# Half of the pooling branch's gates as a third unit of seven products; two recurrence chunks on the un-normalised input; the input's sums later in the list

## The chip, the core and the metric

The kernel runs on one core of a Trainium2 chip. The metric is the device time of one launch in microseconds (us); the kernel before has a median of 901.03 us over three runs (900.64 to 901.3). A core has a matmul engine (TensorE, PE in the profile, with PEld for its weight loads), a vector engine (VectorE, DVE), an engine for activation functions (ScalarE, ACT), a general one (GpSimd, POOL), a queue engine (SyncE, SP) and DMA engines. Each works through a list of its own in order; semaphores hold them together.

## The reference, cut

One layer of a hybrid encoder for 512 tokens of width 1024, all in float32:

```
h = rms_norm(x, norm_mix)
u_pool, u_lru, q, k, v, g_logits = split(h @ w_in)            # 5 x 1024 and 3 x 1024 columns
gates = sigmoid(g_logits + b_gate)                            # three branches x 1024
y_pool = causal means of u_pool over windows 2, 4, 8, 16, less the token, a linear map per group
xc = conv_b + sum_k conv_w[k] * u_lru[t - 3 + k]              # RG-LRU
r = sigmoid(xc @ w_rg + b_rg); i = sigmoid(xc @ w_ig + b_ig)  # block-diagonal
log_a = -8 * r * softplus(-lambda); a = exp(log_a); b = sqrt(-expm1(2 * log_a)) * (i * xc)
y_lru[t] = a[t] * y_lru[t-1] + b[t]
y_sb = stick-breaking attention of 8 heads on rms-normed q, k and on v
merged = sum over branches: gates[branch] * (y_branch @ w_branch[branch])
x = x + merged @ w_out
x = x + (silu(n @ w_ffn_gate) * (n @ w_ffn_up)) @ w_ffn_down,  n = rms_norm(x, norm_ffn)
```

rms_norm scales each token by one number. That number can be left out of a product with `w_in` and multiplied to the result after.

## The kernel before

Channels lie on the 128 partitions and tokens along the rows, so a chunk of 256 output channels is one PSUM pair of tiles 128 x 512. Each float32 operand is split in two parts of fewer bits (`hi` rounded by a ScalarE copy, `lo` the VectorE difference), and each product is three matmuls: hi x hi, hi x lo, lo x hi. `hu` is the input times `norm_mix` in two parts, not yet normalised; `HH` and `HL` (`hn`) are the two parts of the normalised h. `rb` is the row of the tokens' scales, broadcast over partitions.

Weights come in a fixed list, `specs`. A direct chunk of 256 columns has two entries, one for each half of the contraction, with 24 matmuls of 512 columns each. `split_w` takes a raw tile to `whi` (ScalarE, line 110) and `wlo` (VectorE, line 111), three buffers each: the split of entry n needs all matmuls of entry n - 3 done. A Tile scheduler writes each engine's list from the program's order and from priorities (`EARLY`, `AHEAD`); `keep_in_program_order` fixes an instruction against that. PSUM has four pairs of tiles (`pb`).

The stages are:

1. Gates of branch 0 (pooling), chunks 0 and 1, on `hu`, while the input lands; then its chunks 2 and 3, also on `hu`, while the scales and `hn` are made (`norm_h`). Their PSUM results are multiplied by `rb` and go through a sigmoid (`gate_store`).
2. The recurrence. `lru_chunk(c)` is 48 matmuls on `hn` (`ps_lru`), a convolution over time on VectorE, a split of its result, 12 matmuls `lg` with the two small matrices, eight sigmoids on ScalarE (`lr`, `li`), then tanh, exponential and square root (`lru_exp`), and on VectorE `lru_decay`, `lru_input`, `lru_scan`, `lru_store`. Four such chunks stand between the direct gate chunks of branch 1, `gate1(0..3)`. The small pieces are put in a list `bg` by `step`, and each half of a chunk's matmuls takes pieces from it by `tick`.
3. V, K, Q by seven products of half size instead of eight (Winograd's form of Strassen). `ORDER` is the order of the seven, and T1 to T4 are the sums of blocks of h that they need (`diff_h`, then `split_t`, parts `hT1h` and so on; `prepare_t` lists these eight steps). Product 11 of V lands in `ps_q`; ScalarE takes a snapshot `r` of it (`snap`, line 811), and S2 then adds onto the same PSUM tile.
4. Gates of branch 2 by seven products, two units of 512 channels each: 7 x 24 matmuls of 256 columns (`product`, line 287, `gate_done`), from the same sums T1 to T4. Weights of these units are held in eight buffers `qw`, and sums of them are made by accumulating DMAs and VectorE.
5. Pooling, attention and the branches' projections, which read the gates back from DRAM; the output projection; the FFN.

The work behind stage 4 isn't touched, but for the address from which the first branch reads two chunks of gates.

## Time and profile before

| | |
|---|---|
| three runs | 900.64, 901.03, 901.3 us |
| profiled execution | 900.73 us, of it 899.0 us from the first to the last instruction |
| TensorE's granted clock | 1.000 |
| TensorE busy | 893.4 us of the span, 99% |
| VectorE busy | 732.3 us, 81% |
| ScalarE busy | 523.2 us, 58% |

A line of the profile's timeline reads: start in us, length in us, engine, line of the kernel, operation, output<-inputs, shapes, xcount, and in brackets the idle time before it and what ended that. `whi<-raw` is a weight split. A matmul's length holds its way through the array, so the pitch between starts is what it costs. Groups of neighbouring alike instructions may be shown as one line with a count.

### The profile page before, as it was taken

To read this page: it belongs to the slowest core of one execution; us is meant where nothing else is said; L and a number is where in the kernel's file an instruction comes from. 1 tells how busy PE (TensorE), PEld (TensorE's weight loads), DVE (VectorE), ACT (ScalarE), POOL (GpSimd) and SP (SyncE) were. 2 spreads that over 40 slices of the span, in tenths; PEclk is the share of its full clock that TensorE was granted. 3 is DMA by queue.
4 is the path that set the end of the run, shared out by engine and by line. 5 is a ranking of instruction groups with operands and counts; after the bars stand their busy time and mean duration, and the time that the engine had idled before them with its cause. 6 is when DMAs were issued, how large, how long until landed. Compare 5 with 4: busy or idle time off the path is not lost.

```text
span 899.0 us, 14052 instructions
## 1 busy us (share of the span) xinstructions
PE 893.4 (99%) x5491; PEld 794.2 (88%) x5491; DVE 732.3 (81%) x922; ACT 523.2 (58%) x722; POOL 86.3 (10%) x126
## 2 busy tenths in 40 slices
PE   9999999999999999999999999999999999999998
PEld 6888778788899888888888988889999999989998
DVE  7897897988786599967887696699888888799764
ACT  7554989556856556555664544454555555664532
POOL 1110002232332101000001100000000000101200
PEclk9999999999999999999999999999999999999999
DMA  9585347789682785734736865245543333866842
GB/s 337 147 303 156 115 127 215 234 286 242 181 260 71 233 235 190 220 118 141 223 91 152 184 177 170 94 131 152 141 117 95 111 102 125 225 167 122 180 99 94
DMA packets 116579, 151.98 MB, mean 169 GB/s; under 512 B 8096, under 2 KB 90016, under 8 KB 116512
## 3 DMA queue, kind: packets, MB, share of 16 engines
q1 hardware_dynamic: 104416, 107.30, 37.7%
q0 software_dynamic: 11952, 43.52, 20.6%
q8 instruction: 43, 0.70, 0.3%
q10 hardware_dynamic: 144, 0.26, 0.1%
q14 instruction: 24, 0.20, 0.1%
HBM read 130.61 MB, written 18.87 MB: 166 GB/s over the span
## 4 chain that ended last, share of the span: by engine, by line
PE 95%; DVE 2%; ACT 2%; issue 1%; DMA 0%; SPq 0%; DVEq 0%; ACTq 0%
PE ps_y L287 11%; PE ps_x L287 8%; PE ps_q L798 7%; PE ps_dy L287 5%; PE ps_dx L287 4%; PE ps_br L278 3%; PE ps_br L279 3%; PE ps_br L280 3%; PE ps_gate L701 2%; PE ps_bY L1238 2%; PE ps_gy L287 2%; PE ps_gate L280 2%; PE ps_bX L1238 2%; PE ps_gx L287 2%; PE ps_gate L279 2%; PE ps_gate L278 2%
## 5 line engine op out<-in xcount | busy, mean ns | idle before, releaser
L110 ACT ACTIVATE whi<-raw 128x1024 fp32r<-128x1024 f32 x73 | 77.2, 1058 | 85.3 <-PE ps_out L279 17.0
L111 DVE TENSOR_TENSOR wlo<-raw,whi 128x1024 fp32r<-128x1024 f32 x73 | 89.1, 1220 | 32.9 <-ACT whi L110 32.9
L111 DVE TENSOR_TENSOR wlo<-qw,whi 128x1024 fp32r<-128x1024 f32 x48 | 58.6, 1222 | 20.8 <-ACT whi L110 20.5
L110 ACT ACTIVATE whi<-qw 128x1024 fp32r<-128x1024 f32 x48 | 50.8, 1057 | 33.1 <-PE ps_q L798 18.6
L1403 ACT ACTIVATE wh_S<-w_S 128x1024 fp32r<-128x1024 f32 x36 | 38.2, 1064 | 35.5 <-PE ps_y L287 22.4
L1404 DVE TENSOR_TENSOR wl_S<-w_S,wh_S 128x1024 fp32r<-128x1024 f32 x36 | 43.8, 1220 | 6.2 <-ACT wh_S L1403 6.2
L1403 ACT ACTIVATE wh<-w 128x1024 fp32r<-128x1024 f32 x27 | 28.8, 1066 | 30.3 <-issue 11.9
L1494 POOL DMA_DIRECT2D dw<-in_w_down_dram x16 | 13.5, 846 | 325.9 <-DVE wl L1404 248.2
L1404 DVE TENSOR_TENSOR wl<-w,wh 128x1024 fp32r<-128x1024 f32 x27 | 32.9, 1220 | 10.0 <-ACT wh L1403 10.0
L1403 ACT ACTIVATE whdS<-dw 128x1024 fp32r<-128x1024 f32 x16 | 17.0, 1064 | 24.4 <-PE ps_dy L287 13.2
L1404 DVE TENSOR_TENSOR wldS<-dw,whdS 128x1024 fp32r<-128x1024 f32 x16 | 19.6, 1224 | 12.9 <-ACT whdS L1403 12.9
L1054 DVE TENSOR_TENSOR_SCAN E<-K,ahead 128x512 f32<-128x512 f32 (+3 forms) x32 | 25.3, 812 | 4.4 <-ACT K L1050 4.4
L278 PE MATMUL ps_br<-yHH,whi 128*128 128x512 f32 x64 | 25.3, 395 | 0.0
L278 PE MATMUL ps_lru<-HH,whi 128*128 128x512 f32 x64 | 25.2, 394 | 0.0
L278 PE MATMUL ps_br<-yph,whi 128*128 128x512 f32 x64 | 25.2, 394 | 0.0
L278 PE MATMUL ps_pool<-HH,whi 128*128 128x512 f32 x64 | 25.2, 393 | 0.0
L279 PE MATMUL ps_br<-ypl,whi 128*128 128x512 f32 x64 | 25.0, 391 | 0.0
L280 PE MATMUL ps_gate<-HH,wlo 128*128 128x512 f32 x64 | 25.0, 391 | 0.0
L278 PE MATMUL ps_gate<-HH,whi 128*128 128x512 f32 x64 | 25.0, 391 | 0.0
L280 PE MATMUL ps_br<-yph,wlo 128*128 128x512 f32 x64 | 25.0, 391 | 0.0
L279 PE MATMUL ps_br<-yHL,whi 128*128 128x512 f32 x64 | 25.0, 390 | 0.0
L279 PE MATMUL ps_pool<-HL,whi 128*128 128x512 f32 x64 | 25.0, 390 | 0.0
(717 smaller groups left out, 3426.3 us busy)
## 6 DMA issues: line engine op xcount, KB each, us to landing
raw<-in_w_in_dram SPq DMA_DIRECT2D x31, 512.0 KB, 5.2
qw<-in_w_qkv_dram SPq DMA_DIRECT2D x24, 512.0 KB, 6.8
w<-in_w_ffn_gate_dram SPq DMA_DIRECT2D x36, 256.0 KB, 4.1
w<-in_w_ffn_up_dram SPq DMA_DIRECT2D x36, 256.0 KB, 4.6
raw<-in_w_branch_dram SPq DMA_DIRECT2D x16, 512.0 KB, 4.4
dw<-in_w_down_dram POOLq DMA_DIRECT2D x16, 512.0 KB, 6.3
qw<-in_w_qkv_dram POOLq DMA_DIRECT2D x12, 512.0 KB, 7.6
qd<-r POOLq DMA_DIRECT2D x12, 512.0 KB, 7.2
```

The lines of the kernel that those rows point to most:

```text
L110: act(hi, raw, AF.Copy)
L111: dve.tensor_tensor(lo, raw, hi.bitcast(F32), ALU.subtract)
L278: nc.tensor.matmul(ps, lh, rh, start=start, stop=False, skip_group_check=skip)
L279: nc.tensor.matmul(ps, lh, rl, start=False, stop=False, skip_group_check=skip)
L280: nc.tensor.matmul(ps, ll, rh, start=False, stop=stop, skip_group_check=skip)
L287: nc.tensor.matmul(o, a_[a][:, w, k, :], b_[b][:, k, :], start=first and n == k == 0, stop=last and n == 2 and k == 3, skip_group_check=True)
L701: nc.tensor.matmul(pss[n // 2][n % 2], w[:, k % 2, n * P:(n + 1) * P], hu[k][x_], start=k == 0 and w is wh and x_ == 0, stop=k == KT - 1 a ...
L798: nc.tensor.matmul(ps[:, a, :], b_[:, k, ts_], a_[:, kk, :], start=first and n == k == 0, stop=n == 2 and k == 3, skip_group_check=True)
L1054: dve.tensor_tensor_scan(E[:, c0:c0 + n][:, ::-1], K[:, c0 + 1:c0 + n + 1][:, ::-1], ahead[:, S - n:][:, ::-1], 0.0, ALU.mult, ALU.add)
L1238: nc.tensor.matmul(o, ah[x_][:, w, k, :], b[k][y_], start=first_ and n == k == 0, stop=n == 2 and k == 3, skip_group_check=True)
L1403: act(h, src, AF.Copy)
L1404: dve.tensor_tensor(l, src, h.bitcast(F32), ALU.subtract)
```

## The change

The gates of branch 0 in chunks 2 and 3 are no longer made directly. They become a third unit of seven products behind the two of branch 2 (`UNITS`, `GATES`, `gd2[2]`, the third part of `w_gate7`, which is laid out before the launch). The two recurrence chunks 0 and 1 stand in their place and take `hu`; their PSUM result is multiplied by `rb` on VectorE into a tile `un` (`late_rms`), and the convolution reads that. Their convolution and split no longer have priority `EARLY`. Chunk 2 stands where chunk 0 stood, on `hn`, and ScalarE copies it from PSUM to `un` (line 610). The eight steps of `prepare_t` (`tq`), which stood as a block behind the pieces of the recurrence, go singly into the steps between, and the sums are kept in program order; in the list before, the scheduler had placed them earlier than the program did. The diff:

```diff
@@ -149,7 +149,8 @@
-    UNITS = [(t, 2, (2, 512)) for t in VKQ] + [(3 + cc, 1, (2, 4, P)) for cc in range(2)]
+    UNITS = [(t, 2, (2, 512)) for t in VKQ] + [(3 + n, 1, (2, 4, P)) for n in range(3)]
+    GATES = ((2, 0), (2, 1), (0, 1))
...
@@ -188,7 +189,7 @@
                 if un < 3:
                     seven_load(un + 1, {"S1": ("21",), "S3": ("11",), "S4": ("12",), "22": ("22",)}.get(nm, ()))
-                elif un == 3:
+                else:
...
@@ -200,8 +201,6 @@
-    for c in range(2, 4):
-        add_gate(0, c)
...
@@ -387,9 +386,9 @@
-          for br in range(2) for c in range(4)}
-    gd2 = {(cc, j): dr.tile([P, 2, S], F32, tag=f"gd2{cc}{j}", name=f"gd2{cc}{j}")
-           for cc in range(2) for j in range(2)}
+          for br in range(2) for c in range(2 + 2 * br)}
+    gd2 = {(n, j): dr.tile([P, 2, S], F32, tag=f"gd2{n}{j}", name=f"gd2{n}{j}")
+           for n in range(3) for j in range(2)}
...
@@ -517,10 +516,12 @@
         def diff_h(nm, a, sign, b):
-                    dve.tensor_tensor(o, p_, q_, ALU.subtract)
+                    d = dve.tensor_tensor(o, p_, q_, ALU.subtract)
-                    dve.scalar_tensor_tensor(o, p_, -1.0, q_, ALU.mult, ALU.subtract)
+                    d = dve.scalar_tensor_tensor(o, p_, -1.0, q_, ALU.mult, ALU.subtract)
+                tc.keep_in_program_order(d)
...
@@ -594,12 +595,21 @@
         def lru_chunk(c):
-            pair = chan_chunk(("lru", c), hn, 1, pb, True)
-            u, xc = pair, b4([2, S], f"xc{c}")
+            late_rms = c < 2
+            u = chan_chunk(("lru", c), hu if late_rms else hn, 1 if c else 2, pb, True)
+            xc = b4([2, S], f"xc{c}")
             with tc.high_priority(EARLY):
+                if late_rms:
+                    pair, u = u, b4([2, S], f"un{c}")
+                    for j in range(2):
+                        dve.tensor_tensor(u[:, j, :], pair[:, j, :], rb, ALU.mult)
+                elif c in (2,):
+                    pair, u = u, b4([2, S], f"un{c}")
+                    act(u, pair, AF.Copy)
                 for j in range(2):
-                    dve.tensor_scalar(xc[:, j, :], pair[:, j, :], vcol("conv_w", 24 + 2 * c + j),
+                    dve.tensor_scalar(xc[:, j, :], u[:, j, :], vcol("conv_w", 24 + 2 * c + j),
...
@@ -638,7 +648,7 @@
             def early(f):
-                with tc.high_priority(EARLY):
+                with tc.high_priority(0 if late_rms else EARLY):
                     f()
...
@@ -707,12 +717,7 @@
         bg.extend([lambda n=n: norm_h(n) for n in range(4)])
-        pss.append(chan_chunk(("gate", 0, 2), hu, 2, pb))
-        bg.append(lambda: gate_store(0, 2, pss[2], False))
         bg.extend([lru_constants, load_lru_weights])
-        pss.append(chan_chunk(("gate", 0, 3), hu, 2, pb))
-        gate_store(0, 3, pss[3], False)
-        tick(len(bg))
...
@@ -732,15 +737,15 @@
         c2, s2, g2, t2 = lru_chunk(2)
         step(of(lru_exp, (0,))), step(c2), step(s2), step(g1)
         gate1(0)
-        step(of(lru_decay, 0), t1), step(of(lru_exp, (1,))), step(g2), step(of(lru_input, 0))
+        tq = prepare_t()
+        step(of(lru_decay, 0), t1), step(of(lru_exp, (1,)), tq[0], tq[1]), step(g2, tq[2]), step(of(lru_input, 0), tq[3])
         c3, s3, g3, t3 = lru_chunk(3)
-        step(c3), step(s3), step(of(lru_decay, 1), of(lru_scan, 0)), step(t2, of(lru_input, 1))
+        step(c3, tq[4]), step(s3, tq[5]), step(of(lru_decay, 1), of(lru_scan, 0)), step(of(lru_input, 1), tq[6])
         gate1(1)
-        step(of(lru_scan, 1)), step(g3, of(lru_store, 0)), step(t3, of(lru_store, 1)), step(of(lru_exp, (2, 3)))
+        step(of(lru_scan, 1)), step(g3, t2, of(lru_store, 0), tq[7])
+        step(t3, of(lru_exp, (2, 3)), of(lru_store, 1)), step()
         gate1(2)
-        for f, c in ((lru_decay, 2), (lru_decay, 3), (lru_input, 2)):
-            step(of(f, c))
-        bg.extend(prepare_t())
+        step(of(lru_decay, 2), of(lru_input, 2)), step(of(lru_decay, 3))
         gate1(3)
...
@@ -847,12 +852,12 @@
                 act(t[:, w, :], t[:, w, :], AF.Sigmoid, scale=-1.0 if j else 1.0,
-                    bias=vcol("b_gate", 16 + 2 * (2 * cc + w) + j))
+                    bias=vcol("b_gate", 8 * GATES[cc][0] + 2 * (2 * GATES[cc][1] + w) + j))
-        for cc in range(2):
+        for cc in range(3):
-            if cc:
+            if cc == 2:
...
@@ -988,7 +993,8 @@
             gts = [slot_ld(f"g{br}{c}{j}") for j in range(2)]
             for j in range(2):
-                nc.sync.dma_start(gts[j], gd[br, c][j * P:(j + 1) * P, :])
+                nc.sync.dma_start(gts[j], gd2[2, j][:, c % 2, :] if br == 0 and c > 1 else
+                                  gd[br, c][j * P:(j + 1) * P, :])
...
@@ -1648,7 +1654,8 @@
-    lay["w_gate7"] = wi[:, 7168:].reshape(2, 4, P, 2, 2, 2, P).transpose(3, 5, 0, 2, 4, 1, 6)
+    wg = _np.concatenate([wi[:, 7168:], wi[:, 5632:6144]], 1)
+    lay["w_gate7"] = wg.reshape(2, 4, P, 3, 2, 2, P).transpose(3, 5, 0, 2, 4, 1, 6)
```

What the scheduler makes of it is seen in the lists. TensorE's has 5355 rows before and 5427 after. The first place is TensorE around the first `lg` matmuls of the recurrence's chunk 0, before; `ps_lru_707` is the third chunk of the recurrence:

```order
L280 MATMUL ps_lru_707<-HH_105,wlo_677 128x512
L626 MATMUL lg_768<-xch_668,lwh 128x512 x2
L626 MATMUL lg_768<-xcl_669,lwh 128x512 x2
L626 MATMUL lg_768<-xch_668,lwl 128x512 x2
L626 MATMUL lg_779<-xch_668,lwh 128x512 x2
L626 MATMUL lg_779<-xcl_669,lwh 128x512 x2
L626 MATMUL lg_779<-xch_668,lwl 128x512 x2
L278 MATMUL ps_lru_707<-HH_105,whi_676 128x512
L279 MATMUL ps_lru_707<-HL_107,whi_676 128x512
```

After; here `ps_lru_579` is the third chunk, and the first on normalised input:

```order
L279 MATMUL ps_lru_579<-HH_105,wlo_546 128x512
L636 MATMUL lg_640<-xch_537,lwh 128x512 x2
L636 MATMUL lg_651<-xch_537,lwh 128x512 x2
L277 MATMUL ps_lru_579<-HH_105,whi_545 128x512
L636 MATMUL lg_640<-xcl_538,lwh 128x512 x2
L636 MATMUL lg_640<-xch_537,lwl 128x512 x2
L636 MATMUL lg_651<-xcl_538,lwh 128x512 x2
L636 MATMUL lg_651<-xch_537,lwl 128x512 x2
L278 MATMUL ps_lru_579<-HL_107,whi_545 128x512
```

In both, `lg` stands after 36 of the third chunk's 48 matmuls; after, the two gate chunks of stage 1 don't stand ahead of it, and the `xcl` pairs come one matmul later.

The second place is ScalarE at the same point, around the first sigmoids of the recurrence (`lr` and `li` from `lg`), before:

```order
L110 ACTIVATE whi_710<-raw_708 128x1024
L110 ACTIVATE whi_752<-raw_750 128x1024
L630 ACTIVATE lr_672<-lg_768,vt 64x512
L631 ACTIVATE li_673<-lg_768,bigx 64x512
L630 ACTIVATE lr_672<-lg_768,vt 64x512
L631 ACTIVATE li_673<-lg_768,bigx 64x512
L630 ACTIVATE lr_672<-lg_779,vt 64x512
L631 ACTIVATE li_673<-lg_779,bigx 64x512
L630 ACTIVATE lr_672<-lg_779,vt 64x512
L110 ACTIVATE whi_812<-raw_810 128x1024
L631 ACTIVATE li_673<-lg_779,bigx 64x512
L638 ACTIVATE lt_802<-lr_672,cpos 128x512 x2
```

And after:

```order
L110 ACTIVATE whi_624<-raw_622 128x1024
L110 ACTIVATE whi_686<-raw_684 128x1024
L640 ACTIVATE lr_541<-lg_640,vt 64x512
L641 ACTIVATE li_542<-lg_640,bigx 64x512
L640 ACTIVATE lr_541<-lg_640,vt 64x512
L110 ACTIVATE whi_726<-raw_724 128x1024
L641 ACTIVATE li_542<-lg_640,bigx 64x512
L640 ACTIVATE lr_541<-lg_651,vt 64x512
L641 ACTIVATE li_542<-lg_651,bigx 64x512
L640 ACTIVATE lr_541<-lg_651,vt 64x512
L641 ACTIVATE li_542<-lg_651,bigx 64x512
L648 ACTIVATE lt_674<-lr_541,cpos 128x512
```

Before, one split stands among the eight sigmoids, behind the seventh; after, `whi_686` stands right ahead of the first and `whi_726` behind the third. `whi_686` needs the matmuls with `whi_545` done, the second half of the third chunk, and `whi_726` those with `whi_582`, the first half of the gate chunk that follows.

The third place is ScalarE where the sums of the input are split. Before, they stand ahead of all sigmoids:

```order
L110 ACTIVATE whi_600<-raw_598 128x1024
L527 ACTIVATE hT1h<-hT_1264 128x1024
L527 ACTIVATE hT3h<-hT_1301 128x1024
L110 ACTIVATE whi_634<-raw_632 128x1024
L527 ACTIVATE hT4h<-hT_1313 128x1024
L110 ACTIVATE whi_676<-raw_674 128x1024
L110 ACTIVATE whi_710<-raw_708 128x1024
```

After, they stand among the sigmoids of the recurrence's chunks 2 and 3 (`lg_862`, `lg_1024`), and `hT4h` twelve rows behind `hT3h`:

```order
L641 ACTIVATE li_747<-lg_862,bigx 64x512
L528 ACTIVATE hT2h<-hT_830 128x1024
L110 ACTIVATE whi_1061<-raw_1059 128x1024
L528 ACTIVATE hT1h<-hT_827 128x1024
L571 ACTIVATE gt_987<-ps_gate_1_896,vt 128x512 x2
L528 ACTIVATE hT3h<-hT_873 128x1024
L640 ACTIVATE lr_941<-lg_1024,vt 64x512
L641 ACTIVATE li_942<-lg_1024,bigx 64x512
```

From the first `lg` sigmoid up to the snapshot `r` of V's product 11, ScalarE's list holds 85 instructions before and 90 after: four splits of sums, one `un` copy and one `whi` more, one Identity (`lt<-lt`) less.

## The prediction

> **What bounds the kernel now.** I read the page first, then the list of TensorE's waits, the windows of 20 us over the stage that the change rebuilds, and the timelines of TensorE and ScalarE there. The page's first part, its clock row and its chain:
>
> ```profile
> span 899.0 us, 14052 instructions
> PE 893.4 (99%) x5491; PEld 794.2 (88%) x5491; DVE 732.3 (81%) x922; ACT 523.2 (58%) x722; POOL 86.3 (10%) x126
> PEclk9999999999999999999999999999999999999999
> PE 95%; DVE 2%; ACT 2%; issue 1%; DMA 0%; SPq 0%; DVEq 0%; ACTq 0%
> ```
>
> TensorE is busy for 893.4 of 899.0 us at full clock and carries 95% of the chain. Its list of waits over the whole run has three entries:
>
> ```profile
> PE warm_ps L422 <- DVE warm L301: 1.5, 1, 1.5
> PE ps_gate L701 <- ACT hu L437: 0.5, 1, 0.5
> PE ps_q L798 <- DVE wlo L111: 0.4, 1, 0.4
> ```
>
> So no engine gives way today: matmuls taken out are time won, if the others keep up. Whether they do is read from the stage. The windows (columns: busy time and instructions of TensorE, weight loads, VectorE, ScalarE, GpSimd, then clock, DMA share, GB/s):
>
> ```profile
> 60.00:80.00 20.00, 20.00 (x89) 16.33 (x87) 20.00 (x26) 5.20 (x5) 0.89 (x1) 1.00 0.78 244
> 80.00:100.00 20.00, 20.00 (x98) 15.77 (x98) 14.85 (x18) 18.38 (x23) 0.00 (x0) 1.00 0.36 105
> 100.00:120.00 20.00, 20.00 (x94) 16.04 (x93) 15.59 (x18) 19.68 (x25) 0.76 (x1) 1.00 0.24 79
> 120.00:140.00 20.00, 20.00 (x92) 15.73 (x92) 15.73 (x15) 17.47 (x25) 2.95 (x5) 1.00 0.74 250
> 140.00:160.00 20.00, 20.00 (x88) 16.23 (x88) 16.64 (x15) 17.90 (x21) 3.53 (x5) 1.00 0.55 145
> 81.04:153.28 72.24, 72.24 (x332) 57.32 (x329) 55.05 (x57) 68.76 (x86) 6.19 (x9) 1.00 0.46 140
> ```
>
> ScalarE is at 58% over the run, but from 80 to 160 us, where all four recurrence chunks' sigmoids, tanhs, exponentials and roots lie, it is at 18 to 19.7 of 20. That is the number on which I rest. The marks of the stage on TensorE (gates (0,2) begin; first normalised chunk; first `lg` product of the recurrence; V; the product S2 of V; its one wait):
>
> ```profile
> 27.33 0.39 PE L278 MATMUL ps_gate<-hu,whi 128*128 128x512 f32 x1
> 50.02 0.39 PE L278 MATMUL ps_lru<-HH,whi 128*128 128x512 f32 x1
> 80.03 0.50 PE L626 MATMUL lg<-xch,lwh 64*128 64x512 f32 x2
> 144.58 0.39 PE L798 MATMUL ps_q<-whi,HH 128*128 128x512 f32 x1
> 155.76 0.39 PE L798 MATMUL ps_q<-whi,hT2h 128*128 128x512 f32 x1
> 167.39 0.50 PE L798 MATMUL ps_q<-wlo,hT3h 128*128 128x512 f32 x1 [0.36 <-DVE wlo L111]
> ```
>
> And on ScalarE: two splits that wait for matmuls, the first sigmoid, two later waits, the snapshot `r` of V's product 11, which S2 overwrites:
>
> ```profile
> 71.75 1.06 ACT L110 ACTIVATE whi<-raw 128x1024 fp32r<-128x1024 f32 x1 [4.33 <-PE ps_lru L279]
> 77.19 1.06 ACT L110 ACTIVATE whi<-raw 128x1024 fp32r<-128x1024 f32 x1 [4.38 <-PE ps_lru L279]
> 81.04 0.69 ACT L630 ACTIVATE lr<-lg,vt 64x512 f32<-64x512 f32 x1 [2.79 <-PE lg L626]
> 95.32 1.06 ACT L110 ACTIVATE whi<-raw 128x1024 fp32r<-128x1024 f32 x1 [0.27 <-PE ps_gate L279]
> 126.42 1.06 ACT L110 ACTIVATE whi<-raw 128x1024 fp32r<-128x1024 f32 x1 [2.24 <-DVE li L635]
> 153.28 1.03 ACT L811 ACTIVATE r<-ps_q 128x1024 f32<-128x1024 f32 x1
> ```
>
> The snapshot ends at 153.28 + 1.03 = 154.31, only 1.45 us before S2 begins at 155.76. ScalarE is late by almost as much as it can be.
>
> **The change part by part: TensorE's work.** The prices are in the chain (start, length, operation, count):
>
> ```profile
> 249.06 5.44 PE ps_q0S L798 x24
> 262.81 2.84 PE ps_gx L287 x24
> 271.32 2.72 PE ps_gy L287 x24
> ```
>
> 24 matmuls of 512 columns take 5.44 us, 226.7 ns each; 24 of 256 columns take 2.72, exactly half. Two direct gate chunks go: 96 x 226.7 ns = 21.76 us. A third unit of seven products comes: 7 x 24 matmuls, 7 x 2.72 = 19.04 us (7 x 2.84 = 19.88 at the worst row). Balance -2.72, at worst -1.88. The recurrence products are as many as before, on `hu` instead of `HH`.
>
> The Trainium skill ("TensorE: Matmul & The Clock Gate", section "Back-to-back issue gap") speaks against this exchange: it gives a sustained spacing of about 81 ns for 128 columns and 131 for 512, so that a narrow matmul would cost more than its share of columns. By a straight line between these two, an estimate from that page, 256 columns would cost about 75% of 512, and the unit 28.6 us, which makes the exchange +6.8 instead of -2.7. The trace does not agree: its two rows stand at one half, and I go by them.
>
> What the third unit asks of the others is read from the two units that are there:
>
> ```profile
> 259.94:278.98 19.04, 19.04 (x166) 19.04 (x166) 14.20 (x14) 11.19 (x14) 9.23 (x8) 1.00 0.45 129
> 278.98:298.02 19.04, 19.04 (x171) 19.04 (x170) 11.97 (x11) 11.93 (x16) 1.10 (x2) 1.00 0.33 99
> ```
>
> VectorE at 12 to 14.2 and ScalarE at 11.2 to 11.9 of 19.04, with the weights' DMAs and accumulations landing: TensorE never stops there, so I cost seven splits instead of four, and the DMAs, at nothing (if a weight landed late, one product, 2.72). The old wait of 0.36 us at 167.39 I count as gone. TensorE's own sum: -2.72 - 0.36 = -3.08.
>
> **VectorE.** The two scalings of the un-normalised chunks take the place of two scalings of gates:
>
> ```profile
> 33.20 1.28 DVE L568 TENSOR_TENSOR gt<-ps_gate,rb 128x512 f32<-128x512 f32 x2
> ...
> L111 DVE TENSOR_TENSOR wlo<-raw,whi 128x1024 fp32r<-128x1024 f32 x73 | 89.1, 1220 | 32.9 <-ACT whi L110 32.9
> ...
> 27.33:167.39 140.06, 139.69 (x635) 112.76 (x633) 120.02 (x133) 102.59 (x122) 13.62 (x18) 1.00 0.58 180
> ```
>
> The price is the same (1.28 for two). Of the stage's work VectorE loses the four weight subtractions of the two gate chunks, 4 x 1.22 = 4.9 us, and of the 140.06 us from the first of these chunks to the end of the old wait it is idle for 20.0. The stage shrinks by 21.76, so 20.0 + 4.9 - 21.76 leaves some 3 us. I cost it at nothing; what it costs if that cover is gone is the second rival.
>
> **ScalarE, the term that decides.** TensorE holds the same work between the first `lg` product and S2 in both orders: 155.76 - 80.03 = 75.73 us. The first `lg` comes earlier: the order puts it after 36 of the 48 matmuls of the chunk that still begins at 50.02, at 50.02 + 36 x 0.2267 = 58.18, so unhindered V would begin at 58.18 + (144.58 - 80.03) = 122.73 and S2 at 133.91, both 21.85 earlier.
>
> In the same stretch ScalarE does 85 instructions in the order of before and 90 in that of after. Kind by kind these differ in six: one copy of a recurrence chunk out of PSUM (`un`), one more `whi` split, four splits of the sums (`hT1h` to `hT4h`), and one Identity less. Back to back these cost 0.95 to 1.06:
>
> ```profile
> 56.99 1.04 ACT L527 ACTIVATE hT1h<-hT 128x1024 fp32r<-128x1024 f32 x1
> 57.94 1.04 ACT L527 ACTIVATE hT3h<-hT 128x1024 fp32r<-128x1024 f32 x1
> 148.91 1.06 ACT L670 ACTIVATE lt<-lt 128x1024 f32<-128x1024 f32 x1
> 149.87 1.06 ACT L110 ACTIVATE whi<-qw 128x1024 fp32r<-128x1024 f32 x1
> ```
>
> That is 6 - 1 = 5 at about 0.97, +4.85 us. The four splits ran at 55 to 62 us before, where ScalarE has little else (5.2 of 20 busy in the window from 60); now they stand among the sigmoids. Before, the stretch takes 153.28 - 81.04 = 72.24, of it 2.24 + 0.27 in waits: about 69.7 of work. After: 69.7 + 4.85 = 74.6, more than what is left.
>
> It also starts later against TensorE. In the order of after the split `whi_686` stands ahead of the first sigmoid, and its tile comes free only when the running chunk's last matmul is done: 50.02 + 10.88 (48 x 0.2267) + 1.59 for the 12 `lg` matmuls in between (the chain's row below) = 62.49.
>
> ```profile
> 80.10 1.59 PE lg L626 x12
> ```
>
> With 1.06 for the split and some 0.2 for signals the first sigmoid begins at 63.75, 5.6 after its product, where it was 1.01. After three sigmoids of 0.7 (65.85) stands `whi_726`, which needs the next half chunk's end, 62.49 + 5.44 = 67.93: another 2.1 of waiting. A third such split (`whi_1061`) I put at 0.6, in the likeness of the 0.27 and 2.24 above. The snapshot then begins at 63.75 + 74.6 + 2.7 = 141.05 and ends at 142.1, and S2 stands at 142.2 instead of 133.9: 8.3. Laying the two queues against each other by hand, instruction by instruction, gives places where TensorE waits before that (about 1.5 and 1.0 at chunk 2's `lg`, 1.2 at gates (1,1), some 5 in V) and a total of 9.4, since VectorE's part of V comes late as well. I take 9.0. With no wait of ScalarE at all it would be 5.4 (63.6 + 74.6 + 1.1 - 133.9); those are the ends. Behind V, ScalarE is far from full again, so nothing is given back.
>
> **Sum**, against the profiled execution (900.73, span 899.0): 900.73 - 3.08 + 9.0 = 906.65. The median of the runs shown, 901.03, is 0.3 above that execution, less than either end of any term, and I add nothing for it: 906.7.
>
> **The rivals.** *TensorE alone counts (other side, 0.12).* It is busy 99% and waits 2.4 us in all; if ScalarE's lag is swallowed, only matmuls count: 900.73 - 3.08 = 897.65. For it: TensorE's stream runs well ahead of its consumers at four PSUM buffers, and the 69.7 contain gaps between instructions that a fuller queue may close. Against it: the slack of 1.45. The point of decision is whether ScalarE's stretch, start to snapshot, fits into 133.9 - 63.75 - 1.1 = 69 us.
>
> The Trainium skill ("Perfetto Trace Analysis", section "Identifying the Most-Contended Engine") says to find the most contended engine and optimise it first, by occupancy for ScalarE and by the busy share of weight loads for TensorE; over the whole run, 88% against 58%, that is TensorE and gives this rival. Its next section, "Optimization Strategy", adds that the most contended engine can change over time, and the 20 us windows agree with that.
>
> *VectorE falls behind too (0.12).* Some 3 us of idle time over 118 are no cover for work that has to come in order: the sums `hT`, scans and subtractions stand between each other, and each that comes late makes the next split late. Against it: 9 us more of waiting on ScalarE give VectorE 9 us more. With two to four operations of 1.22 late in a row, 3 to 5 us on top: 909.7 to 911.7.
>
> *Half of the lag (0.06).* Only the extra work bites, with the late start hidden behind the PSUM buffers: 4.85 - 1.45 = 3.4, so 901.05, no difference.
>
> *The change doesn't do what it says (0.01).* The order shows the third unit and the moved sums: TensorE's list goes from 5355 to 5427 rows, -96 + 168.
>
> **How the numbers follow.** The forecast has 0.69: 903.0 to 907.1 by the ends of its term, 5.4 and 9.4. The lower rivals reach down to 901 and below; 902 leaves out the first rival and half of the third, and 911 takes in most of the second. That is 902 to 911 for 8 in 10. About 0.2%, 1.8 us, is what a measurement can tell from no change: slower 0.82 (forecast, second rival, and the last one's 0.01), same 0.06, faster 0.12.
>
> **What would show it.** Right: TensorE's waits list `lg`, `ps_gate` and `ps_q` on ScalarE in the first 170 us, 5 to 10 us in all; first `lg` at about 58.2, the first sigmoid near 63.8 behind a `whi` that waited for `ps_lru`; V near 126 to 127, S2 near 142 to 144. The three stages behind V then hold 19.04 more and no wait. Wrong: V near 122.8, S2 near 133.9, no such waits (first rival); waits named for VectorE's `wlo`, `xcl` or `hT` (second); a third unit of much more than 19.04.

## The result and the profile after

The changed kernel takes 908.71 us (median of four runs, 908.61 to 909.05), the kernel before 900.84 beside it: 1.0086 times, 95% interval 1.0074 to 1.0098. It is slower by 7.9 us; 906.7 was forecast. The profiled execution has a span of 906.8 us, 7.8 more than before. Three lines of its page (busy time by engine, the granted clock in 40 slices, the chain by engine):

```profile
PE 896.3 (99%) x5563; PEld 798.0 (88%) x5563; DVE 739.8 (82%) x929; ACT 529.0 (58%) x730; POOL 88.2 (10%) x128
...
PEclk9999999999999999999999999999999999999999
...
PE 94%; ACT 4%; DVE 1%; issue 1%; DVEq 0%; ACTq 0%
```

The page alone looks as before: TensorE at 99%. What differs is that ScalarE has 4% of the chain instead of 2%. The list of TensorE's waits over the whole run says where:

```profile
PE ps_q2S L803 <- ACT whi L110: 2.0, 1, 2.0
PE ps_q2S L803 <- DVE wlo L111: 1.6, 1, 1.6
PE lg L636 <- ACT li L641: 1.5, 2, 0.7
PE warm_ps L421 <- DVE warm L300: 1.5, 1, 1.5
PE ps_gate L277 <- ACT gt L571: 0.8, 1, 0.8
```

A row reads: who waited, for whom, us in all, how often, the longest. The wait at the start (1.5) was there before. The others, 5.9 us, are new: the `lg` products of recurrence chunk 2 wait for chunk 1's sigmoids, gates (1,1) for a PSUM tile, and V's S1 (S2 behind it) for splits. The windows of 20 us (columns as in the prediction) give the stages:

```profile
58.20:80.00 21.80, 21.80 (x104) 16.57 (x104) 17.76 (x25) 13.54 (x18) 0.84 (x1) 1.00 0.44 113
80.00:100.00 20.00, 17.68 (x73) 13.14 (x72) 19.19 (x22) 18.79 (x23) 0.76 (x1) 0.91 0.44 145
100.00:120.00 20.00, 20.00 (x92) 15.53 (x91) 18.53 (x21) 18.83 (x25) 0.75 (x1) 1.00 0.60 208
120.00:140.00 20.00, 19.94 (x88) 16.17 (x87) 15.17 (x14) 19.86 (x25) 2.83 (x5) 1.00 0.26 94
140.00:160.00 20.00, 16.50 (x65) 13.30 (x66) 18.44 (x17) 12.75 (x14) 5.18 (x7) 0.91 0.95 271
```

ScalarE is full up to V while TensorE has gaps of 2.3 and 3.5 us. The row from 58 to 80 shows ScalarE at 13.5 of 21.8, and this is the waste: it idles there and is late for the next 60 us. The seventh column shows what the prediction hadn't looked for: the granted clock is 0.91 in the two windows with gaps. The marks on TensorE (first normalised chunk, first `lg`, V, S2 of V):

```profile
50.78 0.39 PE L277 MATMUL ps_lru<-HH,whi 128*128 128x512 f32 x1
...
59.03 0.73 PE L636 MATMUL lg<-xch,lwh 64*128 64x512 f32 x4
...
128.90 0.39 PE L803 MATMUL ps_q<-whi,HH 128*128 128x512 f32 x1
...
145.02 0.63 PE L803 MATMUL ps_q<-whi,hT2h 128*128 128x512 f32 x1
```

And on ScalarE the splits that wait, the first sigmoid and the snapshot:

```profile
64.20 1.06 ACT L110 ACTIVATE whi<-raw 128x1024 fp32r<-128x1024 f32 x1 [6.89 <-PE ps_lru L279]
65.17 0.67 ACT L640 ACTIVATE lr<-lg,vt 64x512 f32<-64x512 f32 x1
69.29 1.06 ACT L110 ACTIVATE whi<-raw 128x1024 fp32r<-128x1024 f32 x1 [2.06 <-PE ps_gate L278]
99.42 1.06 ACT L110 ACTIVATE whi<-raw 128x1024 fp32r<-128x1024 f32 x1 [0.95 <-PE ps_gate L278]
...
143.30 1.02 ACT L816 ACTIVATE r<-ps_q 128x1024 f32<-128x1024 f32 x1
```

The first sigmoid stands idle behind a split that waits 6.89 us for matmuls. The snapshot ends at 144.32, and S2 begins at 145.02. In shorter windows (TensorE only: busy time, clock, DMA share, GB/s) the clock is seen to halve right behind the gaps:

```profile
86.00:92.00 6.00, 3.96 (x20) 1.00 0.28 87
92.00:94.00 2.00, 1.73 (x5) 0.62 0.09 33
94.00:96.00 2.00, 2.00 (x6) 0.52 0.78 257
96.00:98.00 2.00, 2.00 (x10) 1.00 0.92 288
139.56:144.00 4.44, 0.89 (x3) 0.97 0.85 159
144.00:146.00 2.00, 2.00 (x5) 0.50 1.02 231
```

From 92.3 to 95.7 the pitch of a 512-column matmul is 0.427 us instead of 0.227, and again from 144 to 147.

The time adds up by the pitches of TensorE's matmuls. The three units of gates begin at 248.89, where 259.94 - 21.76 = 238.18 would be without any lag: 10.7 us late. Of these 5.5 are waits (5.9 less the old 0.36), 0.9 is what the first matmuls behind them took beyond their pitch, 3.2 are the two stretches at half clock, 0.85 was there when the first `lg` began, and 0.3 is pitch between `lg` and other matmuls. The three units last 57.6 us where two lasted 38.6, so 19.04 more; 10.7 + 19.04 - 21.76 = 8.0, and behind them 0.2 is won.

### The profile page after: what moved, and what is told of

Read it like the earlier page. It is cut to its first block, busy times and chain, and to the rows that moved or that the text cites. A ratio compares the mean times of both kernels' runs of the same rounds, so it can differ in the third digit from the quotient of the medians.

```text
span 906.8 us, 14233 instructions
## 1 busy us (share of the span) xinstructions
PE 896.3 (99%) x5563; PEld 798.0 (88%) x5563; DVE 739.8 (82%) x929; ACT 529.0 (58%) x730; POOL 88.2 (10%) x128
## 4 chain that ended last, share of the span: by engine, by line
PE 94%; ACT 4%; DVE 1%; issue 1%; DVEq 0%; ACTq 0%
PE ps_y L286 11%; PE ps_x L286 8%; PE ps_q L803 8%; PE ps_dy L286 5%; PE ps_dx L286 4%; PE ps_gy L286 4%; PE ps_br L277 3%; PE ps_br L278 3%; PE ps_br L279 3%; PE ps_gx L286 3%; PE ps_gate L711 3%; PE ps_bY L1244 2%; PE ps_bX L1244 2%; PE ps_pool L278 2%; PE ps_pool L279 2%; PE ps_pool L277 2%
## 5 line engine op out<-in xcount | busy, mean ns | idle before, releaser
L110 ACT ACTIVATE whi<-raw 128x1024 fp32r<-128x1024 f32 x69 | 73.1, 1059 | 91.9 <-PE ps_br L278 14.4
L111 DVE TENSOR_TENSOR wlo<-raw,whi 128x1024 fp32r<-128x1024 f32 x69 | 84.3, 1222 | 32.1 <-ACT whi L110 32.1
L111 DVE TENSOR_TENSOR wlo<-qw,whi 128x1024 fp32r<-128x1024 f32 x54 | 65.9, 1222 | 27.6 <-ACT whi L110 27.4
L110 ACT ACTIVATE whi<-qw 128x1024 fp32r<-128x1024 f32 x54 | 57.1, 1057 | 37.8 <-PE ps_q L803 18.8
L278 PE MATMUL ps_gate<-HL,whi 128*128 128x512 f32 x64 | 25.7, 401 | 0.0
L279 PE MATMUL ps_br<-yHH,wlo 128*128 128x512 f32 x64 | 25.0, 391 | 0.0
```

The lines of the kernel that those rows point to most:

```text
L110: act(hi, raw, AF.Copy)
L111: dve.tensor_tensor(lo, raw, hi.bitcast(F32), ALU.subtract)
L278: nc.tensor.matmul(ps, lh, rl, start=False, stop=False, skip_group_check=skip)
L279: nc.tensor.matmul(ps, ll, rh, start=False, stop=stop, skip_group_check=skip)
```

## The experiments

Three theories were kept apart. Theory 1: ScalarE's list between the first `lg` sigmoid and V's snapshot sets the end, by its work and by the waits that stand in it. Theory 2: VectorE's list does. Theory 3: the loss is the clock. Each run was compared with the kernel before on its chip; ratios are to that. Differences between variants are differences of medians. The kernel before's own median lay between 900.64 and 901.14 us beside them, so half a us between two variants means nothing.

### Ahead of the snapshot one copy less, two splits later, four splits elsewhere, and ScalarE work added to the kernel before

**e_noun**, on the changed kernel:

```diff
-                elif c in (2,):
+                elif False:
```

> The changed kernel, with ScalarE's copy of recurrence chunk 2 from PSUM taken out: VectorE reads PSUM, as in the kernel before. Theory 1 (ScalarE's list between the first lg sigmoid and the snapshot r of V's product 11 sets the end, and each us taken out of it comes back): one instruction of 0.95 us less, so 907.7, and 906 to 907 if with the smaller waits one of the two stretches at half clock goes. Theory 2 (VectorE's list ends last): no gain, 908.7, or slower if reading PSUM costs VectorE more. Theory 3 (the loss is the clock at half speed after waits, whatever made them): 908.7 unless a stretch at half clock goes, then 907.1.

Measured: 906.19 us, 1.006 (1.0045 to 1.0075). One instruction of 0.95 us brought 2.5. The snapshot begins at 140.22 instead of 143.30, and only one stretch at half clock is left. This is theory 1 at the end of its range with the larger gain. Theory 2 allowed no gain and theory 3 only the 1.6 of the stretch; the 0.9 beyond that and the earlier snapshot speak against both, though the interval still reaches theory 3's 907.1.

**e_pin** fixes where two splits stand on ScalarE's list (`issue_after` queues an instruction behind another on its engine); "12" and "13" are the entries of `specs`:

```diff
...
+    PINS = {'12': ('i', 1, 1), '13': ('t', 1)}
...
-            act(hi, raw, AF.Copy)
+            with tc.issue_after(marks[PINS[n]].ins) if n in PINS else nullcontext():
+                act(hi, raw, AF.Copy)
...
+                    marks["i", ct, two] = act(st["i"][q, j, :], ps[o, two, :], AF.Sigmoid, bias=bigx[o, ct:ct + 1])
...
+                    marks["t", ct] = act(st["t"][:, j, :], st["r"][:, j, :], AF.Tanh, scale=cpos[:, ct:ct + 1])
```

> The changed kernel, with the two weight splits that wait for matmuls moved behind the eight sigmoids of recurrence chunk 0 on ScalarE's list (the first of them) and behind its tanh (the second). Nothing else is taken out. Theory 1: the first sigmoid begins near 61 instead of 65.2 and isn't interrupted by the wait of 2.06, so the snapshot is up to 6 us earlier: TensorE's waits of 5.9 us fall to 0 to 1.5 and at least one stretch at half clock goes, 901.5 to 904. Theory 2: VectorE still has its list to do, no more than 2 us come back, 906.7 to 908.7. Theory 3: as theory 1 where a stretch at half clock goes, otherwise below 1 us.

Measured: 905.30, 1.0048 (1.0033 to 1.0063): 3.4 us came back, less than theory 1 had said. ScalarE's timeline shows why: the first sigmoid begins 5 us earlier, but the next split then waits instead.

```profile
60.10 0.68 ACT L643 ACTIVATE lr<-lg,vt 64x512 f32<-64x512 f32 x1 [3.60 <-PE lg L639]
73.92 1.06 ACT L113 ACTIVATE whi<-raw 128x1024 fp32r<-128x1024 f32 x1 [4.07 <-PE ps_gate L281]
139.26 1.02 ACT L819 ACTIVATE r<-ps_q 128x1024 f32<-128x1024 f32 x1
```

Behind the split at 73.92 ScalarE has no wait up to the snapshot, so its end is set by the work alone from there on.

**e_pool**, on the changed kernel:

```diff
-            act(h, BT[nm], AF.Copy)
+            nc.gpsimd.tensor_copy(h, BT[nm])
```

> The changed kernel, with the four copies that split the sums of the input (hT2h, hT1h, hT3h, hT4h) made by GpSimd instead of ScalarE. Theory 1: four instructions of 0.95 us leave ScalarE's list ahead of the snapshot, 3.8 us earlier, and one stretch at half clock may go with them: 903.3 to 905. Theory 2: VectorE's differences wait for GpSimd, which is slower than ScalarE at it, so 908.7 or more. Theory 3: 907 if a stretch at half clock goes, otherwise 908.7.

Measured: 906.07, 1.006 (1.0045 to 1.0075). The gain of 2.6 us is below theory 1's. GpSimd needs 1.05 to 8.64 us for such a copy, VectorE's subtractions beside two of them take 2.03 and 2.05 instead of 1.22, and TensorE then waits for VectorE at chunk 3 (the waits of TensorE, the rows of GpSimd and VectorE):

```profile
PE lg L636 <- DVE xch L625: 2.0, 1, 2.0
```

```profile
95.30 3.16 POOL L528 CAST hT2h<-hT 128x1024 fp32r<-128x1024 f32 x1 [2.45 <-DVE hT L523]
...
112.64 8.64 POOL L528 CAST hT4h<-hT 128x1024 fp32r<-128x1024 f32 x1
```

```profile
98.50 2.03 DVE L529 TENSOR_TENSOR hT2l<-hT,hT2h 128x1024 fp32r<-128x1024 f32 x1 [0.94 <-POOL hT2h L528]
```

Part of the gain was paid to another engine, so this run is weak evidence for either theory.

**b_tanh**, on the kernel before:

```diff
-                    act(st["t"][:, j, :], st["r"][:, j, :], AF.Tanh, scale=cpos[:, ct:ct + 1])
+                    for _ in range(3 if c > 1 else 1):
+                        act(st["t"][:, j, :], st["r"][:, j, :], AF.Tanh, scale=cpos[:, ct:ct + 1])
```

> The kernel before, with the tanh of recurrence chunks 2 and 3 done three times over (the same result): eight more ScalarE instructions at a pitch of 0.61 to 0.66 us, about 5 us, ahead of the snapshot r of V's product 11; nothing else changes. Theory 1: the snapshot had 1.45 us to spare, so S2 comes 3.5 us later, 904.3, and 905.9 if TensorE's wait brings one stretch at half clock; TensorE's list of waits shows ps_q on ScalarE or VectorE. Theory 2: ScalarE is covered by VectorE or has room, below 1 us. Rival of the prediction (TensorE's work alone counts): 900.8.

Measured: 901.46, 1.0005 (0.9996 to 1.0015), a miss for theory 1 as it was put, and on its face for the rival. The snapshot comes only 1.41 us later, which its 1.45 to spare can hold:

```profile
154.69 1.03 ACT L812 ACTIVATE r<-ps_q 128x1024 f32<-128x1024 f32 x1
```

The wait of 2.24 us at 126.4 is gone from ScalarE's list, and the scheduler put one Identity of 0.95 behind the snapshot: 5.0 - 2.24 - 0.95 leaves 1.8, and 1.41 was seen. So the run didn't load the path, and another was needed.

### The third split, the copy, the clock, and ScalarE work behind its wait

**e_pin2** adds one entry to the pins, and **e_pin2n** takes e_noun's edit as well:

```diff
-    PINS = {'12': ('i', 1, 1), '13': ('t', 1)}
+    PINS = {'12': ('i', 1, 1), '13': ('t', 1), '14': ('s', 0)}
...
+                marks["s", c] = act(lru[c]["s"], lru[c]["t"], AF.Sqrt)
```

> The kernel e_pin with a third weight split pinned: the one that waited 4.07 us for a half of the gate chunk stands behind the square root of recurrence chunk 0 instead of ahead of its exponential. Theory 1 (ScalarE's list up to the snapshot sets the end): these 4 us of idle time leave the list, the snapshot comes 3.5 to 4 us earlier than in e_pin (139.26), at about 135.5, so 901.5, or 900 if the stretch at half clock in V goes too. Theory 2 (VectorE's list ends last): below 1.5 us, 904 to 905.3.

Measured for e_pin2: 904.96, 1.0036 (1.0024 to 1.0048), hardly less than e_pin: the snapshot only moved from 139.26 to 138.81, since a later split now waits 3.34 us for recurrence matmuls (`ps_lru`) instead:

```profile
81.42 1.06 ACT L113 ACTIVATE whi<-raw 128x1024 fp32r<-128x1024 f32 x1 [3.34 <-PE ps_lru L281]
```

Each split that is freed runs up to the next half chunk; with three buffers a split can't run further ahead. Theory 1's number was wrong here for the same reason as in e_pin. The five runs show the clock: 902.64 and 903.22 us at a mean granted clock of 1.000, 904.96 and 905.26 at 0.998, 905.36 at 0.996. The program is the same.

> The kernel e_pin2 without ScalarE's copy of recurrence chunk 2 out of PSUM. Theory 1: 0.95 us less on ScalarE's list, so 0.9 us less than e_pin2, or 2.5 less if a stretch at half clock goes with it; below the kernel before's 900.7 if no wait is left in V. Theory 2: the same as e_pin2.

Measured for e_pin2n: 902.25, 1.0014 (1.0005 to 1.0023), 2.7 us less than e_pin2; theory 1 had 0.9, or 2.5 with a stretch at half clock, and eight of the ten runs have a clock of 1.000. Theory 2, no gain, fails. The one wait left in V is now the snapshot itself (TensorE's waits, and ScalarE):

```profile
PE ps_q L806 <- ACT r L819: 2.1, 1, 2.1
```

```profile
137.20 1.03 ACT L819 ACTIVATE r<-ps_q 128x1024 f32<-128x1024 f32 x1
```

**e_vfill**, on the changed kernel, gives TensorE something to do in the gap:

```diff
...
+                if (t, nm) == (VKQ[0], "S2"):
+                    for _ in range(16):
+                        nc.tensor.matmul(bank("S1")[:, 0, :] if "S1" not in ps else ps["S1"][:, 0, :],
+                                         warm[:, 0:P], warm, start=True, stop=True)
```

> The changed kernel, with 16 matmuls that nothing needs (bf16, 512 columns, 0.227 us each, 3.6 us in all) in TensorE's list ahead of V's products S1 and S2, where it waited 2.0 and 1.6 us; they write the PSUM tile that S1 begins afresh. If the stretch at half clock behind these waits comes from TensorE's idleness: the granted clock stays 1.00 there, and the kernel is 1.5 us faster than the changed one with 16 matmuls more, 907.2. If it comes from something else that runs then (DMA at its full share, VectorE): it stays, 908.7, or 909 with the matmuls that are more than the wait.

Measured: 906.84, 1.0067 (1.0054 to 1.008), 1.9 us less than the changed kernel, with 16 matmuls more. The clock stays up behind the gap, and the waits in V are down from 3.6 us to 0.5, which S2 now waits for the snapshot (windows with all engines, then the wait):

```profile
142.00:144.00 2.00, 1.52 (x7) 0.92 (x7) 2.00 (x3) 1.44 (x2) 0.26 (x1) 1.00 1.09 215
144.00:146.00 2.00, 2.00 (x10) 1.64 (x9) 2.00 (x3) 0.01 (x1) 1.06 (x2) 1.00 1.00 344
```

```profile
PE ps_q L803 <- ACT r L816: 0.5, 1, 0.5
```

DMA is at its full share in both windows and VectorE without a gap, so neither of these lowers the clock by itself; what was taken away is TensorE's idleness. But the 1.9 us are not all the filler's. In this execution the stretch at half clock at 92 us is missing too, where nothing was changed and TensorE is busy for only 3.69 of the 6 us from 86. So V already begins at 127.41 instead of 128.90, and the gates behind V begin 2.15 us earlier: 1.5 of these were there ahead of the filler, and it won about 0.7. The last section comes back to this stretch.

**b_tanh3**, on the kernel before:

```diff
-                    act(st["t"][:, j, :], st["r"][:, j, :], AF.Tanh, scale=cpos[:, ct:ct + 1])
+                    for _ in range(5 if c == 3 else 1):
+                        act(st["t"][:, j, :], st["r"][:, j, :], AF.Tanh, scale=cpos[:, ct:ct + 1])
```

> The kernel before, with the tanh of recurrence chunk 3 done five times over (the same result): eight more ScalarE instructions, 4.9 us, all of them behind the wait of 2.24 us at 126.4 that could have swallowed part of b_tanh's. Theory 1: the snapshot comes 4 to 5 us later than 153.28, its 1.45 to spare are used up, TensorE waits 2.5 to 3.5 us in V, and 904 to 905.5 with a stretch at half clock, 903 to 904 without. Rival of the prediction (TensorE's work alone counts): 900.8.

Measured: 907.50, 1.0073 (1.0058 to 1.0088). Five us on ScalarE, behind the wait that had swallowed b_tanh's, cost 6.4 us on a kernel in which TensorE is busy 99%. The rival of the prediction falls. TensorE's waits, and its clock behind them:

```profile
PE ps_q2S L799 <- ACT whi L110: 3.1, 1, 3.1
...
PE ps_q L799 <- ACT r L812: 1.0, 1, 1.0
```

```profile
160.00:162.00 2.00, 1.83 (x4) 0.50 1.03 244
162.00:164.00 2.00, 2.00 (x6) 0.50 1.03 422
164.00:166.00 2.00, 2.00 (x6) 0.54 0.69 283
```

Two splits that stood behind the snapshot before now stand ahead of it, so the waits are 4.1 instead of the 2.5 to 3.5 expected, and the clock stays at half for 6.8 us instead of 3.4.

### One part alone, and what it would take to be faster

**b_tq**, the kernel before with the change's edits to `diff_h` and `prepare_t` alone:

```diff
+                tc.keep_in_program_order(d)
...
-        step(of(lru_decay, 0), t1), step(of(lru_exp, (1,))), step(g2), step(of(lru_input, 0))
+        tq = prepare_t()
+        step(of(lru_decay, 0), t1), step(of(lru_exp, (1,)), tq[0], tq[1]), step(g2, tq[2]), step(of(lru_input, 0), tq[3])
...
-        bg.extend(prepare_t())
```

> The kernel before with one part of the change alone: the sums of the input are held in program order and go singly into the steps between the recurrence chunks, so that their four splits stand among the sigmoids. TensorE's work is the same. Theory 1 (ScalarE's list up to the snapshot sets the end): 89 instructions instead of 85 ahead of the snapshot, 3.8 us more, of which the wait of 2.24 us at 126.4 and the 1.45 to spare can swallow all or part: 901 to 901.5 if both do, 903 to 904.5 if only the 1.45 does, with a stretch at half clock at the upper end. Theory 2 (VectorE): its list gets easier between 50 and 80 us, where it had no gap, so 900.7 or less.

Measured: 901.83, 1.0009 (1.0000 to 1.0018). The snapshot begins at 155.54, 2.3 us later than before, of which 0.5 was there at the first `lg`, and ends at 156.57; S2 begins at 156.62. TensorE's one wait in V is the old one for a subtraction, 0.5 instead of 0.4. The late sums alone use up all that ScalarE had to spare, and cost nearly nothing while there is something to use up.

**e_cover**, on the changed kernel without the third unit:

```diff
-    UNITS = [(t, 2, (2, 512)) for t in VKQ] + [(3 + n, 1, (2, 4, P)) for n in range(3)]
+    UNITS = [(t, 2, (2, 512)) for t in VKQ] + [(3 + n, 1, (2, 4, P)) for n in range(2)]
...
+    for c in (2, 3):
+        add_gate(0, c)
...
         gate1(3)
+        for c in (2, 3):
+            gate_store(0, c, chan_chunk(("gate", 0, c), hn, 1, pb), True)
```

> The changed kernel without the third unit of seven products: the two gate chunks are direct again, 96 matmuls of 512 columns on the normalised input, behind the last gate chunk of branch 1 and ahead of V. TensorE has 2.72 us more work and 21.76 us more of it ahead of V. Theory 1: V's waits (3.6 us) and the stretch at half clock behind them (1.6) go, since the snapshot has 21.76 us more to come in; the waits at 86 to 92 us (2.3) and their stretch (1.6) stay: 908.7 - 5.2 + 2.7 = 906.2. If the changed order of the steps costs the time whatever lies ahead of V: 911.4.

Measured: 904.84, 1.004 (1.0027 to 1.0054): 3.9 us less with 2.72 us more of TensorE's work. V waits no longer; the waits at 86 to 92 us are the same as in the changed kernel:

```profile
PE lg L638 <- ACT li L643: 1.5, 2, 0.8
PE ps_gate L279 <- ACT gt L573: 0.9, 1, 0.9
```

In three of its four runs the clock stays at 1.000, so those waits alone don't always bring the half clock; with 1.6 off, the expected 906.2 is 904.6. Ahead of V, 21.76 us of direct gate work had been ScalarE's cover.

**e_best2**, on e_pin2n:

```diff
-            if c < 2:
+            if c < 3:
                 dve.tensor_scalar(t, t, -1.0, 1.0, ALU.mult, ALU.add)
...
                 elif nm == "S2":
                     snap((0, 1), ps["11"])
+                    if t == VKQ[0]:
+                        with tc.issue_after(marks["snap", t, (0, 0)].ins):
+                            tq[6](), tq[7]()
...
-                    for f, c in ((lru_input, 3), (lru_scan, 2), (lru_scan, 3), (lru_store, 2), (lru_store, 3)):
+                    for f, c in ((lru_store, 0), (lru_store, 1), (lru_input, 3), (lru_scan, 2), (lru_scan, 3), (lru_store, 2), (lru_store, 3)):
```

> The kernel e_pin2n with five more instructions taken out of ScalarE's list ahead of the snapshot, none left out of the kernel: the stores of recurrence chunks 0 and 1 go behind V's product S3, the splits of T3 and T4 behind the snapshot, and the last step of chunk 2's decay is done by VectorE. Theory 1: 84 instructions, 5 x 0.95 us less than e_pin2n, the snapshot at about 132.5 instead of 137.2, which is early enough: no wait in V, 902.25 - 2.2 = 900.0, down to 899 if the smaller waits go too, so below the kernel before by 0.1 to 0.2%. Theory 2: VectorE's weight subtractions in V end last instead, 901 to 902.

Measured: 903.35, 1.0021 (1.0012 to 1.003), slower than e_pin2n and than both theories had said. The work did leave ScalarE's list: it is ready for the snapshot at 133. But the snapshot's buffer isn't, since with the two stores put off it is the one of a gate whose DMA is still under way (ScalarE's waits):

```profile
ACT r L819 <- DMA gd<-gt: 4.0, 1, 4.0
```

**e_best3** takes the last edit of e_best2 back, and keeps the other two:

```diff
...
-                    for f, c in ((lru_store, 0), (lru_store, 1), (lru_input, 3), (lru_scan, 2), (lru_scan, 3), (lru_store, 2), (lru_store, 3)):
+                    for f, c in ((lru_input, 3), (lru_scan, 2), (lru_scan, 3), (lru_store, 2), (lru_store, 3)):
```

> The kernel e_pin2n with the splits of T3 and T4 behind the snapshot and the last step of chunk 2's decay on VectorE, as in e_best2, but with the stores of recurrence chunks 0 and 1 where they were, so that the snapshot's buffer doesn't wait for a gate store's DMA (the 4.03 us in e_best2). Theory 1: about 2.3 us less than e_pin2n ahead of the snapshot, which then comes at 135, about when TensorE gets to S2: no wait of more than 0.5 us in V, 900.0 to 900.4, 0.1% below the kernel before. If another buffer or VectorE ends last in its place: 901.5 to 902.3.

Measured: 900.10, 0.999 (0.9981 to 0.9999), the only version below the kernel before, by 0.9 us. Its waits, and its snapshot:

```profile
PE warm_ps L424 <- DVE warm L303: 1.5, 1, 1.5
PE lg L639 <- DVE xcl L629: 1.0, 1, 1.0
PE ps_gate L714 <- ACT hu L439: 0.4, 1, 0.4
```

```profile
134.21 1.04 ACT L819 ACTIVATE r<-ps_q 128x1024 f32<-128x1024 f32 x1
```

The snapshot ends at 135.25 and S2 begins at 135.66. The interval only just excludes no change, and 0.9 is a third of the exchange's 2.72: the new wait for `xcl` takes 1.0, the rest was not taken apart. So the exchange pays at all only when ScalarE is out of the way.

## Why the prediction was right

**TensorE's sum.** The third unit was costed at 19.04 and took it:

```profile
287.47:306.51 19.04, 19.04 (x170) 19.04 (x169) 11.69 (x10) 11.92 (x15) 1.09 (x2) 1.00 0.31 99
```

VectorE (11.7) and ScalarE (11.9) were hidden, and no weight landed late. Half of 512 columns is half of the price, as the rows of before had said; the estimate of 28.6 us, worked out from two figures of the Trainium skill ("TensorE: Matmul & The Clock Gate", "Back-to-back issue gap"), doesn't hold for this stream.

**ScalarE's lateness.** The mechanism was right, place by place. From the first sigmoid to the snapshot ScalarE took 143.30 - 65.17 = 78.13 us, of it 2.06 + 0.95 + 0.27 + 0.61 in waits: 74.2 of work, where 74.6 was worked out. The wait among the first sigmoids was put at 2.1 and was 2.06. The first sigmoid came 6.1 us behind the first `lg`, with 5.6 forecast: 4 of the 12 `lg` matmuls have a recurrence matmul between them and the rest, and the split's wait ended half a us later. The waits of later splits were put at 0.6 and were 1.83; they wait for gate matmuls that were late themselves. V began at 128.90 (126 to 127 forecast), S2 at 145.02 (142 to 144). One reading was off without harm: from 80 to 160 us the windows of before show ScalarE busy for 17.5 to 19.7 of 20, not 18 to 19.7.

**What was mis-sized** is the term of 9.0 us. TensorE's waits, with what the first matmuls behind them took, are 5.9 + 0.9 = 6.8, not 9: 1.5 instead of 2.5 at chunk 2's `lg`, 0.8 instead of 1.2 at gates (1,1), 3.6 instead of 5 in V. The rest of the lateness is half clock, 3.2 us, which the prediction had not in its sum, 0.85 from before the first `lg`, and 0.3 of pitch. So 2.2 too much and, less the 0.2 won behind the gates, 4.2 too little partly cancel, and that the forecast was only 2 us off is in part luck. Nor are waits and clock independent: without either stretch, in e_vfill, the gates behind V began 2.15 us earlier and not 3.2, and S2 still waited 0.5 for the snapshot.

The 0.85 us are not the change's. The first `lg` comes at 58.2 to 59.0 in the variants, whose lists are the same up to there. Of the 0.85, 0.76 is there when stage 1's first two gate chunks end (28.09 instead of 27.33). In both executions the first matmul starts at 1.46 us, but the granted clock first rose at 4.12 in that of before and at 7.16 in that of after, and between these two times fall 12 matmuls in the one and 8 in the other.

**What stood last in front of S2.** The snapshot ended at 144.32 and S2 began at 145.02, so it wasn't the snapshot itself. In TensorE's list matmuls of S1 stand ahead of S2, and one of them waited for VectorE, whose subtraction `wlo` ended at 143.94 behind ScalarE's split of 141.88:

```profile
144.00 0.79 PE L803 MATMUL ps_q2S<-wlo,hT1h 128*128 128x512 f32 x1 [1.56 <-DVE wlo L111]
```

This matmul and the next ran at half clock. Without VectorE's lateness and without the half clock S2 could have begun at 144.32 and no earlier, so ScalarE's list set where S2 stands, as forecast, and the other two came on top with 0.7 us at most.

**The rivals.** That TensorE alone counts is refuted by b_tanh3. VectorE ended last for 1.6 us in V, but by the above it was worth 0.7 us or less there; with ScalarE relieved (e_best3) VectorE's `xcl` has the one wait that is left behind the start, 1.0. Half of the lag was not seen. What the chances did not allow for is the clock, and the range held it only because it had room at the top for VectorE.

**What isn't settled.** Of e_noun's 2.5 us, 0.95 is the instruction and up to 1.6 the clock; how the rest of its earlier snapshot (3.1 us) divides between less waiting and a shorter list was not taken apart. The late sums were run alone (b_tq), and the change without the third unit (e_cover), but not the change without the late sums; e_pool comes nearest to it.

## What to carry to other kernels

Read the slack of the second engine at the place where the first needs it, not its share over the run: ScalarE was at 58%, with 1.45 us to spare at one snapshot, and everything that shortens the first engine's work ahead of such a place is taken from that slack. An instruction that waits for a buffer, put ahead of a long run of work on an in-order engine, costs that engine the wait, and freeing it often hands the wait to the next one; look at the whole stretch up to the point of need. A busy matmul engine can also pay for a gap twice, by the gap and by the clock behind it.

## What the runs showed of the hardware

In the changed kernel, after gaps of 0.7 to 2 us that left TensorE idle for 2 to 4 us in all, its granted clock was 0.50 for about 3.4 us, at a pitch of 0.427 us instead of 0.227: some 1.6 us lost each time. In b_tanh3, after waits of 3.1 and 1.0, it was 0.50 for 6.8 us. The Trainium skill ("TensorE: Matmul & The Clock Gate", "What's actually happening") gives a window of 3413 ns for this and says that it runs free of the kernel. The traces agree on both. The profiler records each change of the granted clock: in all 14 traces the changes behind the first rise come at whole multiples of 3.413 us after it. The first matmul starts at 1.46 us in every one of them, but the first rise comes anywhere from 4.12 (before) to 7.16 (after). So the windows lie differently against the kernel in each execution, and the same gaps can fall into one window or be shared out over two:

| execution, one window (us) | TensorE busy, of 3.41 | granted clock in the next window |
|---|---|---|
| after, 89.08 to 92.50 | 1.85 | 0.50 |
| e_vfill, 88.05 to 91.46, the same waits | 2.34 | 1.00 |
| e_cover, 87.64 to 91.06, the same waits | 2.50 | 1.00 |
| after, 140.28 to 143.70 | 0.50 | 0.50 |
| b_tanh3, 155.61 to 159.02 | 0.34 | 0.50 |
| e_pin2, 134.76 to 138.17 | 1.48 | 1.00 |

So the same waits can bring the half clock in one execution and not in another, and one program can take 902.64 or 905.36 us (e_pin2). The last row shows that the busy share of one window is not the whole rule. Nor was it tested why all four runs of the changed kernel have a mean clock of 0.996, two stretches, while four of e_vfill's five have 1.000. Single gaps much shorter than the window were enough, if several came close together. Matmuls that nothing needs filled a wait in V and kept the clock up there (e_vfill).

GpSimd took 1.05, 2.04, 3.16 and 8.64 us for copies of the same shape, 128 x 1024. VectorE's subtractions beside two of them took 2.03 and 2.05 us instead of 1.22, and those beside the longest 1.21 (e_pool).
